# Forgetting attention: fill steps held to places between the heads, and the value product in exact high and low parts with both parts of the values in one stationary operand

## The chip, the core and the metric

The kernel runs on one core of a Trainium2 chip. The metric is the device time of one execution in microseconds; the median of several runs is compared. Engines are named as in the profile: PE (TensorE), DVE (VectorE), ACT (ScalarE), POOL (GpSimd), and SP, whose queue issues nearly all the loads.

## The reference, cut to what matters

One inference step of a decoder with two layers, for a prompt of 512 tokens and for eight samples of four new tokens each. Layer 0 is a state-space layer with sliding-window attention; layer 1 is the forgetting attention that this document is about. Each layer ends with a cross attention to 256 memory tokens and a feed-forward part. All is float32, model width 1024, 16 query heads in four key-value groups, 64 numbers a head.

```python
def fox_attend(q, k, v, cum, q_off):
    # Queries sit at key indices q_off..q_off+Tq-1; logit[t,s] += cum[t]-cum[s].
    ...
    bias = cq[..., :, None] - c[..., None, :]
    mask = jnp.arange(tk)[None, :] <= (q_off + jnp.arange(tq))[:, None]
    return gqa_attend(q, k, v, mask=mask, bias=bias)   # softmax(q k / 8 + bias) v

def fox_prompt(q, k, v, logf):
    cum = jnp.cumsum(logf, axis=1)
    ...  # blocks of 128 queries against all earlier keys

# the samples: 1024 earlier tokens, gathered by page, then the 4 new ones
kp = cache_fox_k[li, page_table].reshape(bs, past, FOX_KV_HEADS, HEAD_DIM)
vp = cache_fox_v[li, page_table].reshape(bs, past, FOX_KV_HEADS, HEAD_DIM)
```

## The kernel before

The whole network is recorded as one program for one core. A matrix product in full precision is made of exact parts: an operand is split into a high part (cast to the matmul's faster type, called fp32r in the profile) and a low part (the difference), and two or three products of the parts are summed in a bank of PSUM. `linear` and `linear_steps` do this for the weights: `pieces` loads a weight piece of 128x1024 on SP into a `room` tile (L158) and splits it, high part on ACT (L162), low part on DVE (L163), into a `split_t` tile.

In layer 1, `odd()` first makes keys, values and the queries of key-value groups 0 and 1 (four of the eight steps of the query projection). Then comes the stage that changes. It has two halves `m`, each with four blocks `c` of 128 queries, and in each block eight heads (`r` two key-value groups, `i` four query heads): 64 heads. Block c looks at W = 128(c+1) keys. A head goes like this:

- PE: two matmuls 128xW give the scores (`kh,qst` and `kl,qst`; the second half of the key rows carries the forget bias).
- DVE: a fused mask, negate and minimum from PSUM into `prt` (L1160).
- ACT: the exponential with its sum (L1161). DVE: the reciprocal (L1162). POOL: the scaling (L1163).
- Two heads later (FOX_AHEAD = 2), PE transposes the weights, c+1 times 128x128 (L141), and DVE or ACT in turn evict them to `PT` (L1143).
- After the block's last head the value product is made: float32 matmuls with 64 columns of V as the stationary operand and 512 columns of `PT` moving, for each key block and for r = 0, 1, the two r in the two column halves of the array. DVE copies the bank to `q` (L1150).

Around the heads, three generators give other work, a step at a time: "q", the other eight half-steps of the query projection (24 matmuls each, and an eviction at L456); "s", the samples' attention in four groups of two samples (`fox_sample`: 16 loads of 128 KB of keys, `fox_k`, and 16 of values, `fox_v`, for each group, at L1237, with the page numbers read by SP at L1233; scores by matmuls of 32 columns; softmax; transposes; value product); and "m", the keys and values of the cross attention's memory (`mem_begin` splits the memory at L251 and L252, then `mem_k` and `mem_v`). FOX_PLAN says after which head which generator takes a step. The order on each engine is then made by a scheduler, which may move work of a later step ahead of a head, or the other way round; `after()` adds an order of two instructions by hand.

PSUM banks have tags: "sc" (two buffers) for scores, "tr" (three), "tp" (two) for transposes, "pv" (one) for the value product. After the heads follows the output projection with `wo_d`; `hold` and `whold` keep its first splits and weight loads behind the eviction of the sixth block (`pvs[5]`).

Of the kernel before, what the change touches and what calls it, by code (L numbers as in the profile page):

```python
# [19 lines left out]
P = 128  # L20
# [19 lines left out]
FOX_PLAN = {}  # L40
for _a, _heads in (("q", range(4, 33, 4)), ("s", [33,34,36,38,40,41,43,45,47,49,51,53,55,57,59,61]), ("m", range(34, 64, 4))):
    for _h in _heads:
        FOX_PLAN[_h] = FOX_PLAN.get(_h, "") + _a
# [63 lines left out]
class Net:  # L107
    def __init__(self, nc, tc, ctx, I, O):
        self.nc, self.tc, self.ctx, self.I, self.O = nc, tc, ctx, I, O
        self.n = self.turn = 0  # L110
        self.hold = self.whold = self.last = None
# [25 lines left out]
    def mm(self, out, lhsT, rhs, start, stop):  # L137
        self.nc.tensor.matmul(out, lhsT, rhs, start=start, stop=stop)  # L138

    def tr(self, out, in_, k=P):  # L140
        self.nc.tensor.transpose(out, in_, self.ident[0:k, 0:k])  # L141

# [328 lines left out]

    def stack_q(self, Q, q, m, tok):

        nc = self.nc
        Q = Q.rearrange("p (r i t) -> p r i t", r=2, i=4)
        for r in range(2):
            a, b = slice(64 * r, 64 * r + 64), slice(64 - 64 * r, 128 - 64 * r)
            src = q.half(m)[a, :, tok]
            nc.scalar.copy(Q[a, r], src)
            nc.vector.tensor_tensor(Q[b, r], src, Q[a, r].bitcast(F32), ALU.subtract)  # L480
        return Q


# [504 lines left out]
    def odd(self, st, nxt, fill):  # L988
        nc, tc, I, O = self.nc, self.tc, self.I, self.O
        with ExitStack() as es:  # L990
# [53 lines left out]
            with tc.tile_pool(name="fox", bufs=1) as fx:  # L1044
                self.pvs = []
# [3 lines left out]
                K2 = self.fox_keys(kT, ncum)  # L1049
                bias = self.fox_bias(fx, klast)  # L1050
# [10 lines left out]
                next(gens["s"])  # L1061
                heads, ahead = 0, []
                for m in range(2):
                    for c in range(4):
                        for _ in self.fox_prompt(q, K2, V, m, c, ahead):
                            heads += 1
                            self.banks = ['sc'] if heads < 33 else ['sc', 'sc', 'tr']
                            for a in FOX_PLAN.get(heads, ""):
                                next(gens[a], None)
                self.fox_turn(ahead, 0)  # L1070
# [16 lines left out]
    def fox_keys(self, kT, ncum):  # L1087
# [20 lines left out]
        mask = self.prt[:, 4736:5248]  # L1108
        self.zero(mask[:, 0:384])
        self.after(nc.gpsimd.tensor_copy(mask[:, 384:512], self.cst[:, C_SWA + 128:C_SWA + 256]), self.last)  # L1110
        return kh, kl
# [13 lines left out]

    def fox_prompt(self, q, K2, V, m, c, ahead):

        nc = self.nc
        W = 128 * (c + 1)
        tok = slice(128 * c, 128 * c + 128)  # L1130
        Q = self.fox_queries(q, m, tok)
        PT = []
        mask = self.prt[:, 5248 - W:5248]

        def turn(pr, r, i):
            if not PT:
                PT.extend(self.H("PT")[:, 0:2048].rearrange("p (k r i t) -> p k r i t", k=2, r=2, i=4) for _ in range(c // 2 + 1))
            tp = self.psum("tp", [P, 4, 128])
            for kb in range(c + 1):
                self.tr(tp[:, kb], pr[:, 128 * kb:128 * kb + 128])  # L1140
            for u in range(c // 2 + 1):
                e = min(2, c + 1 - 2 * u)
                (nc.scalar.copy if i % 2 else nc.vector.tensor_copy)(PT[u][:, 0:e, r, i], tp[:, 2 * u:2 * u + e])  # L1143
            if (r, i) == (1, 3):
                pv = self.psum("pv", [P, 4, 128])
                for kb in range(c + 1):
                    for r in range(2):
                        g = 2 * m + r
                        self.mm(pv[64 * r:64 * r + 64], V[:, kb, 64 * g:64 * g + 64], PT[kb // 2][:, kb % 2, r], kb == 0, kb == c)
                self.pvs.append(nc.vector.tensor_copy(q.half(m)[:, :, tok], pv))  # L1150
        for r in range(2):
            for i in range(4):
                sc = self.bank([P, 512])
                for z in range(2):
                    self.mm(sc[:, 0:W], Q[z][:, r, i], K2[z][:, m, r, 0:W], z == 0, z == 1)
                nm, den, rec = self.ty(1), self.ty(1), self.ty(1)
# [63 lines left out]
    def fox_sample(self, q, kTs, Qb, ncs, V, lf, fx, S, sel):  # L1220
# [3 lines left out]
        keys, vals, page = {}, {}, {}  # L1224
        gate = kd = self.last

# [13 lines left out]
        load(keys, 0, "fox_k")  # L1240
        load(vals, 0, "fox_v")
        yield
        tp = self.psum("tp", [P, 16])
        self.mm(tp[0:32], self.Ub, lf[0:32, 4], True, True)
        nc.vector.tensor_scalar(ncs, tp[0:32].unsqueeze(2).to_broadcast([32, 16, 4]), -1.0, None, ALU.mult)
        self.sample_q(q, Qb)
        for G in range(4):
            sc = [self.psum("sc", [P, 4, 128]), self.psum("sc", [P, 4, 128])]
            sn = self.psum("tp", [P, 32])
            for u in range(2):  # L1250
                self.mm(sc[u].rearrange("p a b -> p (a b)"), sel[:, 128 * (G % 2):128 * (G % 2) + 128], S[:, G // 2, 512 * u:512 * u + 512], True, False)
                for b2 in range(2):
                    for m in range(2):
                        a = 64 * b2 + 32 * m
                        lq = Qb[:, 2 * G + b2, m].rearrange("p r i t -> p (r i t)")
                        self.mm(sc[u][a:a + 32], lq, keys[G, b2][:, 4 * u:4 * u + 4, 128 * m:128 * m + 128], False, True)
            for b2 in range(2):
# [5 lines left out]
                self.mm(sn[a:a + 64], ncs.rearrange("p h t -> p (h t)"), self.ident[0:32, 0:32], False, True)  # L1263
            wk = self.prt[:, 2560:4736]
            pr = wk[:, 0:1056]
            gate = nc.vector.tensor_tensor(pr[:, 1024:1056], sn, c[:, C_MN + 32 * G:C_MN + 32 * G + 32], ALU.add)
            if G < 3:
                load(keys, G + 1, "fox_k")
            yield
            mx, nm, den, d1, rec = self.ty(3), self.ty(1), self.ty(3), self.ty(1), self.ty(1)  # L1270
            for u in range(2):
                nc.vector.tensor_reduce(mx[:, u:u + 1], sc[u].rearrange("p a b -> p (a b)"), AX.X, ALU.max)
            nc.vector.tensor_reduce(mx[:, 2:3], pr[:, 1024:1056], AX.X, ALU.max)
            nc.vector.tensor_reduce(nm, mx, AX.X, ALU.max, negate=True)
            for u in range(2):
                nc.scalar.activation(pr[:, 512 * u:512 * u + 512], sc[u].rearrange("p a b -> p (a b)"), AF.Exp, bias=nm, accum_out=den[:, u:u + 1])
            nc.scalar.activation(pr[:, 1024:1056], pr[:, 1024:1056], AF.Exp, bias=nm, accum_out=den[:, 2:3])
            nc.vector.tensor_reduce(d1, den, AX.X, ALU.add)
            nc.vector.reciprocal(rec, d1)
            yield  # L1280
# [15 lines left out]
            nc.scalar.activation(Osb[:, 0], pv, AF.Copy, scale=rec)  # L1296
            self.sample_o(q, Osb, G, 1)
            if G < 3:
                load(vals, G + 1, "fox_v")
            yield  # L1300


    def mem_begin(self, l):
# [12 lines left out]
        for k in range(KD):  # L1316
            g = self.par[:, G_MEM + 8 * l + k:G_MEM + 8 * l + k + 1]
            self.split(mh, ml, raw[:, k], k, 0, 256, g)
            if first:
                self.square_acc(acc, raw[:, k], k, 256)  # L1320
        if first:
            self.rstd(acc, self.mcol, self.mb, [(0, 0, 128), (1, 128, 128)])
# [381 lines left out]
    def run(self):  # L1704
# [5 lines left out]
        def memory(l):  # L1710
            t = self.mkv = self.H("mkv")
            self.mk, self.mv = t[:, 0:1024].rearrange("p (h k) -> p h k", h=4), t[:, 1024:2048].rearrange("p (b f) -> p b f", b=2)
            nc.gpsimd.memset(t[:, 0:1], 0.0)
            m = self.mem_begin(l)
            yield from self.mem_k(l, m, self.mk)
# [128 lines left out]
```

## Time and profile before

| | |
|---|---|
| median of 3 runs | 1694.12 us (1693.13 to 1695.23) |
| profiled execution | 1698.67 us |
| span in its trace | 1696.9 us |
| mean granted TensorE clock | 0.990 |
| busy, share of the span | PE 97%, DVE 70%, ACT 46%, POOL 19% |
| loaded and stored | 189.27 MB, mean 112 GB/s |

Busy shares are of the whole program; a matmul's record includes time in which it waits inside the array's pipeline, so a busy PE need not be a fast one. The stage that changes lies between 1003 and 1190 us. In the trace an instruction is named by its line, its output and its inputs: `ps<-PT,odd` is the value product, `ps<-fox_k,odd` a sample's scores, `ps<-room,prt` a transpose. Lines are those of each kernel's own text, so the changed kernel's numbers differ from these.

### The profile page before, as it was taken

The page shows a single profiled execution, that of the slowest core. Times are in us where ns is not written, and L with a number is a line of the kernel's source. Part 1 is how long each engine was busy: PE and PEld are TensorE (multiplying, and loading weights), DVE is VectorE, ACT ScalarE, POOL GpSimd, SP SyncE. Part 2 cuts the span into 40 slices and gives each one's busy share as a digit, 9 for nine tenths or more (in the row PEclk, how much of TensorE's full clock was granted, in tenths as well). Part 3 has the DMA queues.
Part 4 walks back from the last instruction along what each step waited for, and adds up shares of the span by engine and source line. Part 5 has one row for each costly group of instructions (what it writes and reads, how often), then busy time and mean ns, then how long its engine had stood idle before and what let it go on. Part 6 is the DMA issues. An engine that isn't in the chain of part 4 may idle for free.

```text
span 1696.9 us, 32362 instructions
## 1 busy us (share of the span) xinstructions
PE 1645.9 (97%) x12720; PEld 1518.7 (89%) x12720; DVE 1184.0 (70%) x2296; ACT 778.3 (46%) x1603; POOL 328.3 (19%) x510
## 2 busy tenths in 40 slices
PE   6999999998999999999999998998999999999997
PEld 6988899886997999999999996655988999999997
DVE  7667678867766887677766567654567877777663
ACT  5255445344444544444445355544545444444444
POOL 5022312657422310000001203111223100000002
PEclk9999999999999999999999999999999999999999
DMA  5211424126533233232323334554551233223222
GB/s 185 63 55 39 145 82 132 51 91 237 207 100 125 81 113 102 89 103 88 106 75 107 127 116 125 160 174 149 181 178 59 75 113 100 94 100 106 75 68 86
DMA packets 71221, 189.27 MB, mean 112 GB/s; under 512 B 7612, under 2 KB 34012, under 8 KB 63452
## 3 DMA queue, kind: packets, MB, share of 16 engines
q1 hardware_dynamic: 69388, 184.84, 32.9%
q8 instruction: 100, 1.64, 0.4%
q10 hardware_dynamic: 1600, 1.83, 0.4%
q0 software_dynamic: 80, 0.52, 0.1%
q14 instruction: 53, 0.43, 0.1%
HBM read 172.22 MB, written 14.95 MB: 110 GB/s over the span
## 4 chain that ended last, share of the span: by engine, by line
PE 91%; DVE 3%; POOL 2%; ACT 1%; issue 1%; DMA 1%; SPq 0%; DVEq 0%; POOLq 0%; ACTq 0%
PE ps L138 66%; PE ps L1563 22%; PE ps L141 3%; POOL room L425 1%; DMA room<-wo_d 0%; POOL sq L421 0%; DVE split_t L1544 0%; ACT prt L1161 0%; DVE prt L1160 0%; DVE xs L879 0%; ACT split_t L162 0%; DMA mem<-mem 0%; DVE meml L252 0%; DVE x L1730 0%; DMA x<-x 0%
## 5 line engine op out<-in xcount | busy, mean ns | idle before, releaser
L138 PE MATMUL ps<-xh,split_t 128*128 128x288 f32 (+1 forms) x2304 | 463.8, 294 | 13.8 <-ACT split_t L162 11.8
L138 PEld LDWEIGHTS ps<-xh,split_t 128*128 128x128 f32 x2304 | 371.1, 190 | 19.8 <-ACT split_t L162 12.8
L1563 PE MATMUL ps<-xf,split_t 128*128 128x272 f32 x2592 | 348.9, 289 | 3.1 <-DVE split_t L1544 2.1
L138 PE MATMUL ps<-xl,split_t 128*128 128x256 f32 (+1 forms) x1152 | 339.1, 295 | 1.2 <-DVE xl L252 1.0
L1563 PEld LDWEIGHTS ps<-xf,split_t 128*128 128x128 f32 x2592 | 335.0, 188 | 4.4 <-DVE split_t L1544 3.0
L261 POOL TENSOR_TENSOR room<-room,sq 128x256 f32<-128x256 f32 (+1 forms) x96 | 86.4, 904 | 773.4 <-ACT sq L260 771.7
L138 PEld LDWEIGHTS ps<-xl,split_t 128*128 128x128 f32 x1152 | 218.9, 190 | 6.9 <-issue 4.3
L138 PE MATMUL ps<-hh,fs 128*128 128x256 f32 (+1 forms) x1024 | 206.3, 288 | 0.0
L162 ACT CAST split_t<-room 128x1024 fp32r<-128x1024 f32 (+1 forms) x128 | 130.3, 1019 | 156.5 <-PE ps L138 112.3
L163 DVE TENSOR_TENSOR split_t<-room,split_t 128x1024 fp32r<-128x1024 f32 (+1 forms) x128 | 157.0, 1229 | 31.5 <-ACT split_t L162 31.0
L138 PEld LDWEIGHTS ps<-hh,fs 128*128 128x128 f32 x1024 | 164.9, 188 | 0.4 <-ACT fs L1607 0.4
L1544 DVE TENSOR_TENSOR split_t<-fr,split_t 128x1024 fp32r<-128x1024 f32 x108 | 131.7, 1221 | 35.3 <-ACT split_t L1543 35.0
L1543 ACT CAST split_t<-fr 128x1024 fp32r<-128x1024 f32 x108 | 113.4, 1052 | 89.6 <-PE ps L1563 53.4
L138 PE MATMUL ps<-hl,fs 128*128 128x256 f32 (+1 forms) x512 | 147.3, 288 | 0.0
L138 PE MATMUL ps<-oh,split_t 128*128 128x288 f32 (+1 forms) x512 | 105.7, 298 | 1.3 <-ACT oh L246 1.2
L138 PEld LDWEIGHTS ps<-hl,fs 128*128 128x128 f32 x512 | 96.4, 188 | 0.0
L138 PEld LDWEIGHTS ps<-oh,split_t 128*128 128x128 f32 x512 | 83.2, 192 | 8.3 <-issue 5.0
L138 PE MATMUL ps<-ol,split_t 128*128 128x288 f32 (+1 forms) x256 | 77.1, 301 | 0.3 <-DVE ol L249 0.2
L1607 ACT CAST fs<-room 128x512 fp32r<-128x512 f32 x64 | 39.4, 618 | 82.6 <-PE ps L138 68.3
L252 DVE SCALAR_TENSOR_TENSOR xl<-x,room,xh 128x256 fp32r<-128x256 f32 (+1 forms) x96 | 69.6, 755 | 5.6 <-ACT xh L251 5.6
L138 PE MATMUL ps<-hh,split_t 128*128 128x256 f32 (+1 forms) x384 | 73.4, 288 | 0.0
L1620 DVE TENSOR_TENSOR x<-x,ps 128x256 f32<-128x256 f32 (+1 forms) x128 | 54.4, 433 | 26.9 <-PE ps L138 26.7
(423 smaller groups left out, 3091.2 us busy)
## 6 DMA issues: line engine op xcount, KB each, us to landing
fr<-wfi SPq DMA_DIRECT2D x36, 1024.0 KB
room<-wfo SPq DMA_DIRECT2D x64, 256.0 KB
room<-wo_e SPq DMA_DIRECT2D x16, 512.0 KB
xk<-mem_k SPq DMA_DIRECT2D x8, 1024.0 KB
xv<-mem_v SPq DMA_DIRECT2D x8, 1024.0 KB
room<-wfi SPq DMA_DIRECT2D x16, 512.0 KB
fox_k<-fox_k SPq DMA_DIRECT2D x64, 128.0 KB
fox_v<-fox_v SPq DMA_DIRECT2D x64, 128.0 KB
```

Source lines behind the costliest of these rows:

```text
L138: self.nc.tensor.matmul(out, lhsT, rhs, start=start, stop=stop)
L141: self.nc.tensor.transpose(out, in_, self.ident[0:k, 0:k])
L162: nc.scalar.copy(hi[:, 0:n], raw[:, 0:n])
L163: nc.vector.tensor_tensor(lo[:, 0:n], raw[:, 0:n], hi[:, 0:n].bitcast(F32), ALU.subtract)
L252: return nc.vector.scalar_tensor_tensor(ll, src, g, hh.bitcast(F32), ALU.mult, ALU.subtract)
L261: nc.gpsimd.tensor_tensor(acc, acc, sq[:, 0:N], ALU.add)
L425: nc.gpsimd.tensor_tensor(acc, acc, sq, ALU.add)
L1543: nc.scalar.copy(hi, t)
L1544: nc.vector.tensor_tensor(lo, t, hi.bitcast(F32), ALU.subtract)
L1563: self.nc.tensor.matmul(ps, w[a][:, k], x[:, b, k], start=start and k == 0 and i == 0, stop=k == 3 and i == 2, skip_group_check=True)
L1607: nc.scalar.copy(hi, raw)
L1620: nc.vector.tensor_tensor(x, x, ps, ALU.add)
```

## The change

Six edits, all in the forgetting attention:

1. **The plan.** FOX_PLAN has other places: the query steps at heads 2 to 24, the sample's at 8 and 25 to 58, the memory's at 19 to 60. `mem_begin` gives way after every second of its eight splits, in layer 1.
2. **Steps held.** The first PE instruction that a step records is ordered after the latest score matmul (`behind`, `placed`).
3. **Banks.** "tr" may have four buffers, "sc" three, and scores use both tags in all heads. (The scheduler places them in the same eight banks.)
4. **Queries.** The next block's queries are split half a block ahead.
5. **The value product.** V is stacked once as high and low part side by side, 128 columns, one stationary operand for each key block and r (`stack_v`). `PT` is evicted by whole banks into a high part (ACT, a cast) and a low part (DVE, the difference): a bank holds 4, 2, 1, 1 heads for c = 0 to 3. For each block and r, 2(c+1) fp32r matmuls with 512 columns give high and low sums in the two halves of the bank; ACT copies the one half (64x512), DVE adds the other. This is recorded one head later (`late`).
6. **The samples.** Scores go through a fused minimum reduce to SBUF as before in the prompt, and one exponential over 1056 columns takes the place of three. The first keys are loaded at head 8 and not before head 1, the first values at head 25, and the transposed result of a group is put into place a step later. The hold of the output projection is `pvs[11]`, the twelfth of now sixteen evictions.

```diff
-for _a, _heads in (("q", range(4, 33, 4)), ("s", [33,34,36,38,40,41,43,...,59,61]), ("m", range(34, 64, 4))):
+for _a, _heads in (("q", (2, 4, 7, 10, 13, 16, 20, 24)), ("s", (8, 25, 26, 28, 31, 33, ...)), ("m", (19, 21, 23, 25, 35, ...))):
...
-        bufs = {"tr": 3, "sc": 2, "tp": 2, "pv": 1}[tag]
+        bufs = {"tr": 4, "sc": 3, "tp": 2, "pv": 1}[tag]
...
+    def placed(self, i):
+        if self.behind is not None:
+            self.behind, d = None, self.behind
+            self.after(i, d)
+        return i
...
+    def stack_v(self, V, t):
+        ...
+        for r in range(2):
+            nc.scalar.copy(t[:, :, :, r, r], src[:, :, :, r])
+            nc.vector.tensor_tensor(t[:, :, :, r, 1 - r], src[:, :, :, r], t[:, :, :, r, r].bitcast(F32), ALU.subtract)
...
+    def turned(self, PT, tp):
+        self.nc.scalar.copy(PT[0], tp)
+        self.nc.vector.tensor_tensor(PT[1], tp, PT[0].bitcast(F32), ALU.subtract)
+
+    def values(self, q, V2, PT, r, blocks):
+        ...
+        for j, v in enumerate(blocks):
+            for z in range(2):
+                self.mm(pv, v[:, r], PT[z][j], j == 0 and z == 0, j == n - 1 and z == 1)
+        a, b = slice(64 * r, 64 * r + 64), slice(64 - 64 * r, 128 - 64 * r)
+        nc.scalar.copy(q[a], pv[b])
+        return nc.vector.tensor_tensor(q[a], pv[a], q[a], ALU.add)
...
-                self.banks = ['sc']
+                self.banks = ['sc', 'sc', 'tr']
...
+                    for _ in self.fox_prompt(Q, q, K2, V2, m, c, ahead):
+                        heads += 1
+                        if heads % 8 == 4 and j < 7:
+                            nq = ready(*blocks[j + 1])
+                        for a in FOX_PLAN.get(heads, ""):
+                            self.behind = self.scored
+                            next(gens[a], None)
...
-                self.hold = self.whold = self.pvs[5]
+                self.hold = self.whold = self.pvs[11]
```

What it does to the order is shown at three places. First PE, the value product of the last block (`oh`, `ol` is the output projection that runs beside it). Before:

```order
5121 L138 MATMUL ps_13740<-PT_13556,odd 64x512
5122 L141 MATMUL ps_13702<-room,prt 128x128 x4
5133 L141 MATMUL ps_13726<-room,prt 128x128 x4
5134 L141 MATMUL ps_13733<-room,prt 128x128 x4
5135 L138 MATMUL ps_13740<-PT_13556,odd 64x512 x3
5136 L138 MATMUL ps_13740<-PT_13557,odd 64x512 x4
5137 L138 MATMUL ps_13902<-oh_1543_13763,split_t 128x288
```

(between 5122 and 5133 stand matmuls of the output projection and one more set of transposes), and now, for the second half of its heads:

```order
5153 L138 MATMUL ps_13912<-oh_1540_13804,split_t 128x256
5154 L138 MATMUL ps_13783<-PT_13693,Vs_10848 128x512
5155 L138 MATMUL ps_13943<-oh_1538_13794,split_t 128x288
5156 L138 MATMUL ps_13783<-PT_13694,Vs_10848 128x512
5157 L138 MATMUL ps_13783<-PT_13693,Vs_10848 128x512
5158 L138 MATMUL ps_13783<-PT_13694,Vs_10848 128x512
5159 L138 MATMUL ps_13783<-PT_13693,Vs_10848 128x512
5160 L138 MATMUL ps_13783<-PT_13694,Vs_10848 128x512
5161 L138 MATMUL ps_13783<-PT_13693,Vs_10848 128x512
5162 L138 MATMUL ps_13783<-PT_13694,Vs_10848 128x512
```

The first half-width matmul stood alone ahead of the others, and the other seven after the last transposes; now eight full-width ones stand nearly together for this r, and eight more for the other r earlier.

Second DVE, in the last block of the first half (c = 3; L1160 is L1209 now, L1162 is L1211, L1150 is L515, L1143 is L503 and an ACT cast at L502). Before, two heads:

```order
1317 L1160 ISA prt,ty_11959<-ps_11956,prt 128x512
1318 L1160 ISA ty_11959 128x1
1319 L1143 COPY PT_11901<-ps_11966 128x2x128
1320 L1143 COPY PT_11902<-ps_11966 128x2x128
1321 L1162 RECIPROCAL ty_11961<-ty_11960 128x1
1322 L1160 ISA prt,ty_11976<-ps_11973,prt 128x512
```

and now:

```order
1318 L1209 ISA prt,ty_12029<-ps_12026,prt 128x512
1319 L1209 ISA ty_12029 128x1
1320 L503 TENSOR_TENSOR PT_11865<-ps_11983,PT_11864 128x3x128
1321 L1166 CAST qst<-qst 64x512
1322 L1167 TENSOR_TENSOR qst<-q_1102_11137,qst 64x512
1323 L1211 RECIPROCAL ty_12031<-ty_12030 128x1
1324 L503 TENSOR_TENSOR PT_12009<-ps_12010,PT_12008 128x4x128
1325 L515 TENSOR_TENSOR q_1087_10885<-ps_12017,q_1087_10885 64x4x128
1326 L503 TENSOR_TENSOR PT_12009<-ps_12036,PT_12008 128x4x128
1331 L1209 ISA prt,ty_12236<-ps_12233,prt 128x512
```

Every head's transposes now come to DVE as one wide subtract, where every second head's came as copies, and query splits of the next block and sample softmax stand among them.

Third SP, the keys of the second group of samples (group 1) and the memory's value weights (`wxv`). Before:

```order
282 L1237 ISA
283 L1237 DMA fox_k_12256<-fox_k 128x256
284 L158 DMA room<-wxv 128x1024 x2
285 L1237 ISA
286 L1237 DMA fox_v_12474<-fox_v 128x256
```

and now:

```order
250 L1282 TENSOR_LOAD tab_12063
251 L1282 ISA x2
252 L165 DMA room<-wxv 128x1024 x2
253 L1286 ISA
254 L1286 DMA fox_k_12209<-fox_k 128x256
255 L1286 ISA
256 L1286 DMA fox_k_12209<-fox_k 128x256
```

The two weight loads stood behind the sixteen key loads, and stand ahead of them now. Further down, two of the loads of `wo_d` stand behind the first of the last sixteen value loads, where one pair stood behind all of them.

More of the change, by code (lines that the diff above doesn't have):

```diff
@@ L1057, in odd @@
                 self.take(q)
-                self.banks = ['sc']
+                self.banks = ['sc', 'sc', 'tr']
                 gens = {"q": self.linear_steps(wq, range(4, 8), KD, xh, xl, qe),
                         "s": self.fox_sample(q, kTs, Qb, ncs, V, lf, fx, S, sel), "m": fill()}
-                next(gens["s"])
                 heads, ahead = 0, []
[L1063 to L1070, printed above, removed]
+                blocks = [(m, c) for m in range(2) for c in range(4)]
+                ready = lambda m, c: self.fox_queries(q, m, slice(128 * c, 128 * c + 128))
+                Q = ready(*blocks[0])
+                for j, (m, c) in enumerate(blocks):
+                    for _ in self.fox_prompt(Q, q, K2, V2, m, c, ahead):
[5 more added lines that the diff above has]
+                            next(gens[a], None)
+                        self.behind = None
+                    Q = nq
+                for _ in range(FOX_AHEAD):
+                    next(gens["m"], None)
+                    self.fox_turn(ahead, len(ahead) - 1)
                 for a in "qsm":
@@ L1300, in fox_sample @@
             yield
+            self.sample_o(q, Osb, G, 1)
     def mem_begin(self, l):
```

101 lines of the change are left out of this document (57 added, 44 removed).

## The prediction

> **What bounds the kernel now.** I read the page first, then a table of stretches, then the waits of VectorE, then the chain of waits where the forgetting attention ends.
>
> ```profile
> core 0 of [0], span 1696.9 us
> ...
> PE 1645.9 (97%) x12720; PEld 1518.7 (89%) x12720; DVE 1184.0 (70%) x2296; ACT 778.3 (46%) x1603; POOL 328.3 (19%) x510
> ```
>
> TensorE carries the kernel as a whole. But 97% is an average, and PE records are stretched by waits, so I go to the stage that changes. Its 64 heads run in blocks of eight. Each head has one mask-and-min reduce at L1160; the view of that line has the first and the last start after the durations, for all 64 and then for the first heads of the second half (a block of 128 keys, the fifth of eight):
>
> ```profile
> L1160 DVE CUSTOM_DVE_ANT_0 prt<-ps,prt x64: 259/481/692, 1012.0 to 1177.0; 128x128 f32<-128x128 f32 x16, 128x256 f32<-128x256 f32 x16, 128x384 f32<-128x384 f32 x16, 128x512 f32<-128x512 f32 x16
> ```
> ```profile
> L1160 DVE CUSTOM_DVE_ANT_0 prt<-ps,prt x2: 271/276/281, 1068.8 to 1071.0; 128x128 f32<-128x128 f32 x2
> ```
>
> So heads 1 to 32 take 1012 to 1069. The last value product ends at 1186.9 (its row is below). I cut there.
>
> ```profile
> core 0: us, PE busy (x) PEld busy (x) DVE busy (x) ACT busy (x) POOL busy (x), PEclk, DMA share, GB/s
> 1012.00:1069.00 57.00, 52.02 (x323) 37.43 (x322) 43.67 (x152) 34.54 (x98) 18.34 (x37) 1.00 0.44 137
> 1069.00:1187.00 118.00, 110.52 (x872) 72.59 (x864) 64.42 (x217) 57.18 (x159) 17.94 (x33) 0.97 0.54 161
> 1092.00:1112.00 20.00, 18.78 (x114) 12.85 (x110) 11.03 (x38) 9.02 (x24) 2.42 (x5) 0.91 0.67 191
> 1150.00:1172.00 22.00, 17.94 (x159) 11.30 (x157) 11.62 (x37) 11.47 (x33) 2.57 (x4) 0.99 0.65 187
> 1187.00:1240.00 53.00, 51.76 (x408) 51.55 (x409) 33.20 (x55) 25.96 (x49) 15.34 (x16) 1.00 0.45 162
> ```
>
> The last row is the output projection after the heads: 408 matmuls of 256 or 288 columns in 51.76 us, 0.127 us each, or 0.47 ns a column; that is PE at its pace. In the first half of the heads PE starts only 323 matmuls in 57 us, so it is not the limit there, whatever its 52 busy us say. VectorE is the nearest to full, 43.67 of 57, and it takes its work in order. The second half has 64.42 of 118 on VectorE. There PE is the likelier limit, and it loses 118 − 110.52 = 7.5 us to recorded idle and 0.03 × 118 = 3.5 us to a lower granted clock: 11.0 us together.
>
> What VectorE waits for, first half and then second half:
>
> ```profile
> DVE ty L1162 <- ACT prt L1161: 7.0, 13, 1.0
> DVE q L456 <- PE ps L138: 2.7, 2, 1.6
> DVE q L1150 <- PE ps L138: 1.3, 3, 0.7
> ```
> ```profile
> DVE ty L1162 <- ACT prt L1161: 12.1, 18, 2.0
> DVE q L1150 <- PE ps L138: 10.7, 5, 3.8
> DVE PT L1143 <- PE ps L141: 5.8, 6, 1.7
> DVE split_t L163 <- ACT split_t L162: 5.1, 6, 3.3
> DVE mkv L1350 <- PE ps L138: 4.9, 1, 4.9
> ```
>
> In the first half, 7.0 of its 57 − 43.67 = 13.3 idle us are the reciprocal waiting for its own head's exponential: a latency that other work could fill. In the second half the waits are mostly for PE, which is at long pieces of fill.
>
> The chain of waits near the end of the heads:
>
> ```profile
> 1159.19 0.96 SPq L1237
> 1161.29 6.04 DMA room<-wo_d
> 1167.35 1.05 ACT split_t L162
> 1168.43 1.23 DVE split_t L163
> 1170.38 4.43 PE ps L138 x24
> ```
>
> The third load of the output weights is issued behind the last sample values (SPq L1237), and PE waits for it; 1150 to 1172 has 22 − 17.94 = 4.1 us of PE idle.
>
> **The change part by part.** Prices of what the stage does now (by line and shape, 1003 to 1187 us), and of its nearest relatives:
>
> ```profile
> L138 PE MATMUL ps<-PT,odd 128*64 128x512 f32 x80 | 28.6, 618 | 0.5 <-ACT PT L1143 0.5
> L138 PE MATMUL ps<-fox_k,odd 128*32 128x512 f32 x64 | 13.5, 604 | 0.0
> L1143 DVE COPY PT<-ps 128x256 f32<-128x256 f32 x32 | 12.9, 419 | 6.5 <-PE ps L141 6.4
> L1143 ACT COPY PT<-ps 128x256 f32<-128x256 f32 x32 | 11.0, 371 | 27.4 <-PE ps L141 25.9 <-PE ps L138 1.4
> L1143 DVE COPY PT<-ps 128x128 f32<-128x128 f32 x16 | 4.6, 285 | 1.5 <-PE ps L138 1.1 <-PE ps L141 0.3
> L1143 ACT COPY PT<-ps 128x128 f32<-128x128 f32 x16 | 4.2, 261 | 1.3 <-PE ps L141 1.3
> L1150 DVE COPY q<-ps 128x512 f32<-128x512 f32 x8 | 5.5, 692 | 12.0 <-PE ps L138 12.0
> L1272 DVE TENSOR_REDUCE ty<-ps 128x1 f32<-128x512 f32 x8 | 5.5, 689 | 2.8 <-PE ps L138 2.7
> L252 DVE SCALAR_TENSOR_TENSOR meml<-mem,room,memh 128x256 fp32r<-128x256 f32 x8 | 3.4, 466 | 0.0
> ```
> ```profile
> L1421 ACT CAST Ph<-ps x16: 577/586/592, 507.7 to 1284.2; 128x512 fp32r<-128x512 f32 x16
> L1422 DVE TENSOR_TENSOR Pl<-ps,Ph x16: 673/692/693, 509.6 to 1284.9; 128x512 fp32r<-128x512 f32 x16
> ```
> ```profile
> 1183.25 3.65 PE L138 MATMUL ps<-PT,odd 128*64 128x512 f32 x14 [0.46 <-ACT PT L1143]
> ```
> *Evictions of the transposed weights.* Before, VectorE and ScalarE shared them: 12.9 + 4.6 = 17.5 us and 11.0 + 4.2 = 15.2 us. After, every bank is cast by ScalarE and subtracted by VectorE. Banks per key-value head and block: 1, 2, 4, 4 for the four block lengths, so 28 of 512 columns and 16 of 384. The cross attention does just this pair: 0.692 and 0.586 us. For 384 columns I go down by a line from 0.692 to 0.466 at 256 columns: 0.58 us. VectorE: 28 × 0.692 + 16 × 0.58 = 28.7, +11.2 us; ScalarE: 28 × 0.586 + 16 × 0.48 = 24.1, +8.9 us.
>
> *Evictions of the product.* 8 copies (5.5 us) become 16 ScalarE copies and 16 VectorE adds of 64x512. At the 0.692 and 0.586 above: VectorE +5.5 us, ScalarE +9.4 us. Stacking the values (two subtracts, two copies) lies ahead of the heads, where PE is full (the projection of the first queries): 0, at most 1.4 us if that cover is gone.
>
> *The product on PE.* Before, 40 fp32 matmuls of 64 columns, two records each. The last product's trailing 14 records (7 matmuls) take 3.65 us for four pairs of column halves, 0.91 a pair slot. The order puts one half alone ahead in each block, so a block of n key blocks takes n + 1 slots: 28 in all, 25.5 us. After: 80 matmuls 128x512 at 0.47 ns a column, 0.24 each, 19.3 us. Gain 6.2 us, half of it, 3.1, in the second half of the heads; in the first half VectorE hides it. Bounds: no lone slots, 20 × 0.91 = 18.2 us, a loss of 1.1; every record by itself, 28.6 us, a gain of 9.3. The Trainium skill, page "TensorE: Matmul & The Clock Gate", Part 3 on packing, says that matmuls in different column tiles run concurrently, the span being one matmul's duration and about 4 ns for each further tile. That speaks against the change: by it the old halves cost 18.2 us, and my sum would end 3.7 us later. The 80 records of 618 ns sum to 49 us in 28.6 us of PE time, so the trace agrees for the pairs; the order says that not all are pairs.
>
> *Sample scores.* 64 matmuls of 32 columns in 13.5 us, four at a time: 0.84 us a foursome. In the new order the foursomes are broken into twos for three of the four sample groups, before for two: two foursomes more, +1.7 us on PE. The two max-reduces of 0.689 become fused reduces of 512 columns at 0.692: 0.
>
> *Steps moved, first half.* The eight query steps are in heads 1 to 32 in both orders, but eight splits of the memory (0.466 each, 3.7 us) and one more reduce of sample scores (0.7) now come there too. VectorE's additions there: half the weights' 11.2 (5.6), half the product's 5.5 (2.8), 3.7 and 0.7: 12.8 us, 43.67 + 12.8 = 56.5. To this comes idle time: 13.3 at most, as now; about 4 at least, if all the waits for ScalarE (7.0) and for the product (1.3) are filled. I take 7.5, since longer VectorE work between a head's reduce and its reciprocal fills the 7.0 us mostly, while waits for PE stay. So 64 us against 57: **+7.0**, from +3.5 to +12.8. ScalarE then has 34.54 + 9.2 = 44 of 64 and stays covered.
>
> *Steps held, second half.* VectorE has 64.42 of 118; the additions (8.4) less what moved out (4.4) leave it at 68, so it costs nothing there as long as steps are spread. Each step's first PE instruction waits for the latest scores, so behind it queue the later transposes and products on PE; its price is the wait for a score bank, and one more bank each is allowed. What can be won is the 11.0 us of idle and clock; the upper end is 21, an estimate: the forms of the second half at 0.47 ns a column come to some 97 of the 118 us. On SP, two of the output-weight loads now stand behind the first of the last 16 value loads, so the 6-us wait should be out of the chain: 4.1 of the 11. The rest is the clock (0.91 from 1092 to 1112), and gaps that the held steps should split. I take all **11.0**; ends 0 and 21.
>
> Sum: 7.0 − 3.1 + 1.7 − 11.0 = −5.4 us. The profiled execution took 1698.67 (1.8 of it outside the span), 4.6 above the median of the runs; against its own time this gives 1693.3, against the median 1694.12 it gives 1688.7. I say **1688.5**.
>
> **Rivals.**
>
> *VectorE decides throughout (slower).* If the latency is not filled, the first half costs 56.5 + 13.3 = 69.8 us, +12.8. For it: 32 of the 44 banks belong to blocks of 384 and 512 keys, and their subtracts stand in order between the reduces. Then the transposes' bank comes free late, the held steps wait behind it, and the second half wins only the 4.1 of the weights and 1.4 on PE: +7.3, 1701.5. It decides once VectorE's idle time in the first half stays above 12.9 with the full 12.4 won later. Against: in the first half 12.4 us of idle are named waits that more queued work can cover.
>
> *Keys late (slower or same).* The loads of the sample's keys:
>
> ```profile
> 1104.92 15.56 SPq L1237 DMA_DIRECT2D fox_k<-fox_k  x16
> 1133.00 16.13 SPq L1237 DMA_DIRECT2D fox_k<-fox_k  x16
> ```
>
> They take some 16 us where the page numbers are read in between, and in the new order group 1's stand behind two loads of memory weights, of which the second waits for a VectorE split. From their step (head 28) to their use (head 34) are six heads, 6 × 64 / 32 = 12 us. Three groups each 4 us late cost 12, of which the old order had some; I price it at +9: 1697.5.
>
> *The product is no cheaper on PE.* By the concurrent halves: 3.1 + 0.6 us are lost, 1692, no change. *All stalls go:* +3.5 and −21 + 1.7 − 3.1: 1675.
>
> **How the numbers follow.** Forecast 0.36, all stalls 0.10, VectorE 0.24, keys late 0.16, product no cheaper 0.14. A measurement of this kernel tells a change from none at about 0.2%, 3.4 us. Faster: 0.46. Same: the product's case and some of the keys': 0.18. Slower: 0.36. The forecast's own range is 1683 to 1692; with the rivals of both signs 1676 to 1705.
>
> **What would show it.** Right: the 32nd head's reduce some 64 us after the first; the casts and subtracts near 0.586 and 0.692; the second half near 106 us at a granted clock of 0.99; no wait for output weights in the chain. The product right: 80 records spaced near 0.24. Wrong: PE waiting for sample keys (DMA in the waits of L138), VectorE above 90% in either half, ScalarE's copy of the product holding the one product bank, or the second half above 112 us.

## The result, and the profile after

The changed kernel takes 1709.06 us (median of four, 1707.15 to 1713.49) where the kernel before takes 1694.26 (four runs): ratio 1.0097, interval 1.0077 to 1.0116. It is slower by 14.8 us; 1688.5 was forecast, with 1705 as the upper end. Measured again beside other versions it came to 1.0089 (1.0071 to 1.0107), so 0.9% is the size to explain.

The first fence is a line of the changed kernel's page. The second has the first reduces of the second half (first and last start after the durations). The third has the stretches: first half, second half, and the output projection after the heads.

```profile
PE 1644.6 (96%) x12720; PEld 1531.2 (90%) x12720; DVE 1200.3 (70%) x2306; ACT 795.9 (47%) x1601; POOL 329.3 (19%) x510
```
```profile
L1209 DVE CUSTOM_DVE_ANT_0 prt<-ps,prt x2: 272/272/273, 1074.8 to 1075.7; 128x128 f32<-128x128 f32 x2
```
```profile
core 0: us, PE busy (x) PEld busy (x) DVE busy (x) ACT busy (x) POOL busy (x), PEclk, DMA share, GB/s
1009.30:1074.80 65.50, 58.47 (x372) 47.77 (x372) 54.59 (x168) 45.90 (x111) 19.22 (x37) 0.95 0.41 121
1074.80:1197.40 122.60, 104.34 (x827) 76.24 (x827) 69.40 (x209) 61.38 (x140) 18.37 (x33) 0.94 0.52 165
1197.40:1251.00 53.60, 53.10 (x418) 52.65 (x418) 33.40 (x55) 26.54 (x50) 15.35 (x16) 1.00 0.42 138
```

The heads took 57.0 + 118.0 = 175.0 us and take 65.5 + 122.6 = 188.1, 13.1 more. PE's recorded work is the same, 162.5 before and 58.47 + 104.34 = 162.8 now. So nearly all of the 13.1 us is recorded idle time of PE: 175.0 − 162.5 = 12.5 us before, 25.3 now. And the clock is lower: 0.05 × 65.5 + 0.06 × 122.6 = 10.6 us of granted clock are missing, where 3.5 were.

A profile is one execution, and the heads differ between executions. The profiled one of the kernel before, at 1698.67 us, is 4.4 above its median; the bank counts alone, which change nothing in time (e17 below), have heads of 171.9 us in their profile, 56.8 and 115.1. The changed kernel profiled a second time (e12), in an execution 5.9 us above its median, has 192.8:

```profile
1009.30:1077.20 67.90, 61.60 (x381) 50.56 (x380) 54.67 (x167) 46.17 (x111) 18.89 (x37) 0.90 0.38 117
1077.20:1202.10 124.90, 105.37 (x833) 76.73 (x832) 69.53 (x209) 61.35 (x140) 18.22 (x33) 0.95 0.52 162
```

So differences of less than some 5 us between the halves of two profiles below show a direction at most; the ratios decide.

What PE waits for in the second half: matmuls in the first fence, weight loads in the second. "issue" is time for which the profile names no cause.

```profile
PE ps L138 <- DVE ty L1209: 5.2, 8, 2.5
PE ps L138 <- DMA fox_k<-fox_k: 3.4, 3, 2.0
PE ps L141 <- DVE ty L1209: 2.8, 2, 2.4
PE ps L138 <- DVE PT L503: 1.6, 3, 0.8
```
```profile
PEld ps L138 <- issue: 14.7, 25, 2.2
PEld ps L138 <- DVE ty L1209: 8.0, 10, 2.7
PEld ps L138 <- DVE PT L503: 3.7, 5, 1.3
PEld ps L141 <- DVE ty L1209: 3.5, 2, 2.8
```

The same two views of the kernel before, second half, had for the reduce:

```profile
PE ps L138 <- DVE ty L1160: 0.7, 2, 0.5
```
```profile
PEld ps L138 <- DVE ty L1160: 1.9, 5, 0.8
```

The two views overlap in time and are not to be added, but both say the same: PE now waits for VectorE's reduces in the half where it hardly did, and a little for the new subtracts (L503). Over both halves the matmuls' wait for reduces grew less, from 4.8 us before (4.1 of them in the first half) to 10.0.

The row does not say why a reduce is late. Two waits, of 2.46 and 2.40 us, make 4.9 of the 8.0 (5.2 and 2.8) of the second half. The second, with what VectorE did ahead of it:

```profile
1169.90 1.23 DVE L170 TENSOR_TENSOR split_t<-room,split_t 128x1024 fp32r<-128x1024 f32 x1 [1.20 <-ACT split_t L169]
1171.04 0.55 DVE L503 TENSOR_TENSOR PT<-ps,PT 128x384 fp32r<-128x384 f32 x1
1172.32 1.97 PE L141 MATMUL ps<-room,prt 128*128 128x128 f32 x8 [2.40 <-DVE ty L1209]
```

VectorE waited 1.20 us for ScalarE's part of a split of the output weights and split for 1.23 us itself; one subtract of 0.55 us stands behind that, then the reduce. Ahead of the 2.46 (it ends at 1104.71) VectorE had a reduce of sample scores (0.69 us), a weight split (1.22), the split of the next block's queries (0.42 and 0.69) and a wait of 0.24 for the samples' long exponential, and no subtract at all. The longest wait of the first half, 2.59 us for L515, stands behind all eight splits of the memory in a row (3.34 us), though their step gives way after every second one. So the longest waits come from the other work between the heads more than from the subtracts.

The new evictions and the product by shape (1003 to 1198 us):

```profile
L138 PE MATMUL ps<-PT,Vs 128*128 128x512 f32 x80 | 26.0, 441 | 4.2 <-ACT PT L502 2.0 <-DVE ty L1326 1.0 <-DVE PT L503 0.5
...
L503 DVE TENSOR_TENSOR PT<-ps,PT 128x512 fp32r<-128x512 f32 x28 | 18.9, 686 | 1.8 <-ACT PT L502 1.5
...
L502 ACT CAST PT<-ps 128x512 fp32r<-128x512 f32 x28 | 15.9, 583 | 9.8 <-PE ps L141 8.0 <-DMA fox_k<-fox_k 1.6
...
L514 ACT COPY q<-ps 64x512 f32<-64x512 f32 x16 | 9.3, 581 | 15.1 <-PE ps L138 14.9
L503 DVE TENSOR_TENSOR PT<-ps,PT 128x384 fp32r<-128x384 f32 x16 | 8.6, 550 | 0.5 <-ACT PT L502 0.5
```

### The profile page after: what moved, and what is told of

Same layout as the page of the kernel before. It is cut to its first block, busy times and chain, and to the rows that moved or that the text cites. A ratio compares the mean times of both kernels' runs of the same rounds, so it can differ in the third digit from the quotient of the medians.

```text
span 1708.4 us, 32362 instructions
## 1 busy us (share of the span) xinstructions
PE 1644.6 (96%) x12720; PEld 1531.2 (90%) x12720; DVE 1200.3 (70%) x2306; ACT 795.9 (47%) x1601; POOL 329.3 (19%) x510
## 4 chain that ended last, share of the span: by engine, by line
PE 87%; DVE 5%; issue 2%; SPq 2%; POOL 2%; ACT 2%; DMA 1%; DVEq 0%; ACTq 0%; POOLq 0%
PE ps L138 63%; PE ps L1614 22%; PE ps L141 2%; SPq L1286 1%; POOL room L432 1%; SPq L1282 1%; DVE prt L1209 0%; DVE PT L503 0%; ACT split_t L169 0%; POOL sq L428 0%; DVE split_t L1595 0%; DMA mem<-mem 0%; DVE xs L913 0%; DMA room<-wo_d 0%; DVE q L515 0%
```

## The experiments

Each ratio is to the kernel before, measured with it on the same chip. Every edit also lets the scheduler make another order, so a ratio holds the edit and what that does to the order.

| run | what it is | ratio | interval |
|---|---|---|---|
| e1 | before + new product | 1.0083 | 1.0068 to 1.0097 |
| e2 | changed, old product | 1.0025 | 1.0015 to 1.0036 |
| e3 | changed, steps not held | 1.0131 | 1.0114 to 1.0148 |
| e4 | changed, keys in two loads | 1.0107 | 1.0094 to 1.0120 |
| e5 | changed, no subtracts | 1.0046 | 1.0028 to 1.0064 |
| e6 | changed, 40 matmuls for 80 | 1.0080 | 1.0062 to 1.0098 |
| e7 | changed, keys a group earlier | 1.0112 | 1.0092 to 1.0131 |
| e8 | changed, two product banks | 1.0079 | 1.0057 to 1.0101 |
| e9 | e2, memory's steps later | 1.0054 | 1.0034 to 1.0074 |
| e10 | e2, samples' steps later too | 1.0049 | 1.0031 to 1.0067 |
| e11 | changed, high part only | 1.0019 | 1.0002 to 1.0037 |
| e12 | changed, again | 1.0089 | 1.0071 to 1.0107 |
| e13 | before + new samples' part | 1.0290 | 1.0267 to 1.0312 |
| e14 | e2, old bank counts | 1.0177 | 1.0155 to 1.0199 |
| e15 | e2, steps not held | 1.0032 | 1.0019 to 1.0045 |
| e16 | before + new product, high part only | 0.9980 | 0.9965 to 0.9994 |
| e17 | before + new bank counts | 1.0000 | 0.9985 to 1.0014 |
| e18 | e16 + new bank counts | 0.9994 | 0.9980 to 1.0007 |

**The product alone, and everything but the product.** e1 takes `stack_v`, `turned`, `values` and the new `turn` into the kernel before; e2 puts the old `turn` into the changed kernel:

```diff
-            if i % nh == nh - 1:
-                self.turned([t[:, :, i - nh + 1:i + 1] for t in PT], bank[0])
...
+            for u in range(c // 2 + 1):
+                e = min(2, c + 1 - 2 * u)
+                (nc.scalar.copy if i % 2 else nc.vector.tensor_copy)(PT[u][:, 0:e, r, i], tp[:, 2 * u:2 * u + e])
```

> The kernel before with the exact-part value product alone (edit 5: stacked values, whole-bank casts and subtracts, one head later, the hold on the twelfth of sixteen evictions); plan, banks and samples as before. Theory D (the added evictions on VectorE and ScalarE cost the time): the first half of the heads grows from 57 us to about 65, the whole kernel by 8 to 14 us over before, to 1702-1708. Theory K (sample keys late under the new plan) or H (steps held make PE wait): within 3 us of before, since neither the plan nor the holding is in it.

> The changed kernel with the old value product (fp32, 64 columns, copies by both engines, hold on the sixth of eight evictions); plan, held steps, banks, queries and samples as changed. Theory D: about 1697, 12 us below the changed kernel. Theories K and H: 1706 to 1711, no gain, as the keys and the held steps stay.

e1 is 0.83% slower than before, e2 only 0.25%. The product makes most of the loss, in either plan. Halves of e1 and of e2, cut as above:

```profile
1010.20:1070.40 60.20, 50.06 (x319) 41.19 (x321) 49.41 (x151) 42.26 (x103) 18.07 (x37) 0.97 0.36 110
1070.40:1193.30 122.90, 106.45 (x866) 78.17 (x858) 74.26 (x221) 67.23 (x165) 17.85 (x33) 0.94 0.51 155
```
```profile
1004.90:1071.50 66.60, 63.25 (x420) 48.68 (x420) 51.90 (x171) 40.88 (x109) 19.50 (x37) 1.00 0.44 133
1071.50:1183.70 112.20, 100.91 (x780) 63.81 (x778) 56.28 (x202) 48.52 (x131) 17.83 (x33) 0.94 0.51 161
```

The product alone (e1) costs 3.2 us in the first half and 4.9 in the second. The rest of the change alone (e2) costs 9.6 in the first half and wins 5.8 in the second: PE does 420 matmuls in the first half instead of 323, so the steps were moved there and paid for there. Together (the changed kernel) the second half loses the gain and 4.6 more: 10.4 us separate it from e2's. These halves are set against a profile that is 4.4 us above its median, and the 8.1 us of e1 are short of its 0.83%, 14 us; against e17's halves e1 costs 3.4 and 7.8, and e2 costs 9.8 and wins 2.9.

In e1's second half the wait for reduces (L1195 there) is small, and waits for ScalarE lead, for a cast (L496) and for exponentials of the samples (L1311):

```profile
PE ps L138 <- ACT PT L496: 3.3, 1, 3.3
PE ps L141 <- ACT prt L1311: 2.5, 1, 2.5
PE ps L138 <- DVE ty L1195: 1.0, 2, 0.5
```

So the product costs as much where PE hardly waits for reduces in this half. Those waits are not the one chain by which it costs.

**Holding the steps.** The one line that names the score is taken out:

```diff
                         for a in FOX_PLAN.get(heads, ""):
-                            self.behind = self.scored
                             next(gens[a], None)
```

> The changed kernel without the order between a step's first PE instruction and the latest score. Theory H: 8 us or more below the changed kernel, about 1700. Theories D and K: within 3 us of 1709.

> e2 without the order between a step and the latest score. With the new product the holding was worth 6 us (e3 against the changed kernel). If it is worth as much here: 1.0055 or more. If holding only helps where VectorE is late: within 2 us of e2's 1.0025, or below it.

Not holding them is slower (e3), so the holding is not the cause. With the old product it makes no difference that can be measured (e15 against e2). Theory H (the held steps make PE wait) falls.

**Keys.** In e4 the keys of groups 1 to 3 come in two large loads from fixed pages, which leaves out the page table; in e7 they are loaded a group earlier:

```diff
+        load(keys, 1, "fox_k")
...
-            if G < 3:
-                load(keys, G + 1, "fox_k")
+            if G < 2:
+                load(keys, G + 2, "fox_k")
```

> The changed kernel, in which the keys of sample groups 1 to 3 come from fixed pages in two loads of 1 MB each instead of sixteen of 128 KB after sixteen page numbers (it leaves out the page table for these keys). Theory K: 8 to 12 us below the changed kernel, 1697 to 1701, the second half of the heads near 112 us. Theories D and H: within 3 us of 1709.

> The changed kernel with the sample keys loaded one group earlier: groups 0 and 1 ahead, group G+2 once group G's scores are made. Theory K (keys late, 3.4 us of PE waits named for them and more behind): 4 to 8 us below the changed kernel. Theories D2, P, B: within 3 us of 1709.

No gain in either. e4 is no clean test, as its two loads were queued behind others and a wait for keys was left. In e7 the wait for keys is

```profile
PE ps L138 <- DMA fox_k<-fox_k: 2.6, 2, 2.4
```

where 3.4 stood, and the time is not lower. Neither edit takes the wait away, so neither is a clean test. The better evidence is e1 and e2: e1 keeps the old plan and its loads and still loses 0.83%; e2 keeps the new plan and its loads, its PE still waits 2.5 us for keys in the second half, and it loses 0.25%. Keys are late now and then, but they are not the 14 us.

**Inside the product.** e5 drops the 44 subtracts and puts the high part in the place of the low one, e6 drops the 40 matmuls with the low part of the weights, e11 both; e8 gives the product a second bank.

```diff
     def turned(self, PT, tp):
         self.nc.scalar.copy(PT[0], tp)
-        self.nc.vector.tensor_tensor(PT[1], tp, PT[0].bitcast(F32), ALU.subtract)   # e5, e11
...
-            for z in range(2):
-                self.mm(pv, v[:, r], PT[z][j], j == 0 and z == 0, j == n - 1 and z == 1)
+            self.mm(pv, v[:, r], PT[0][j], j == 0, j == n - 1)                         # e6, e11
```

> The changed kernel without the 44 VectorE subtracts that make the low part of the transposed weights; the high part is used in both products (it leaves out the low part, and keeps all 80 wide matmuls and all ScalarE casts). Theory D2 (VectorE's subtracts, in order between a head's reduce and its reciprocal, keep the second half of the heads long): 9 us or more below the changed kernel, 1700 or less. Theory P (the 80 wide matmuls cost PE more than the old product) and B (the one product bank): within 3 us of 1709.

> The changed kernel with half of the product's matmuls: the product with the low part of the weights is left out, 40 matmuls in place of 80; all evictions stay. Theory P: 40 x 0.23 = 9 us below the changed kernel, about 1700. Theory D2: PE is not what is late, at most 3 us below, 1706 to 1709.

> The changed kernel without the low part of the weights at all (it leaves out the 44 subtracts of e5 and the 40 matmuls of e6). If subtracts and matmuls are two prices of one product, it comes to e2's ratio, 1.002 to 1.003; if the matmuls only fill time in which PE waits anyhow, to e5's, 1.0046; if ScalarE's casts and copies (33 us where 15 stood) carry most, it stays above 1.005.

> The changed kernel with two banks allowed for the value product. Theory B (each product waits until ScalarE's copy and VectorE's add of the one before have freed the one bank): 4 us or more below the changed kernel. Theories D2, P, K: within 3 us of 1709.

> The changed kernel itself, as the measure for the others on one chip: 1.0097 of before, within 1.0077 to 1.0116; PE idle near 25 us between the first reduce and the last product, where the kernel before has 12.

From 1.0089 (e12), the subtracts are worth 0.43% (7 us), the matmuls by themselves 0.09%, which the intervals do not tell from nothing; both together 0.70% (12 us). That is e2's ratio, so what is left of the product, with its casts and copies but also with 40 wide matmuls in place of the old 40 of two records each, comes to no more than the old one. Half the wide matmuls, some 9 us of PE, bring next to nothing while the subtracts are there. Halves of e6 and of e11:

```profile
1008.10:1077.40 69.30, 63.20 (x416) 52.48 (x414) 58.23 (x172) 47.96 (x115) 18.25 (x37) 0.93 0.37 115
1077.40:1192.90 115.50, 97.28 (x755) 67.22 (x756) 65.29 (x205) 58.55 (x137) 17.73 (x33) 0.91 0.52 157
```
```profile
1007.10:1071.40 64.30, 59.76 (x407) 49.41 (x407) 48.59 (x154) 47.60 (x114) 19.41 (x37) 0.97 0.46 140
1071.40:1178.60 107.20, 90.44 (x750) 64.44 (x751) 50.99 (x180) 59.19 (x138) 17.71 (x33) 0.95 0.51 158
```

In e6 VectorE has 58.23 + 65.29 = 123.5 us, as much as the changed kernel's 124.0, and the heads take 184.8, of which PE is idle for 24.3 (25.3 in the changed kernel), with 0.07 × 69.3 + 0.09 × 115.5 = 15.2 us of clock missing (10.6). PE's recorded work is 160.5 us for 162.8, so the matmuls left out show neither as time won nor as more idle time. In e11 VectorE has 99.6 us and the heads take 171.5, in an execution of 1691.83 us that is 5.5 below its median. A second product bank (e8) brings nothing that can be measured.

**The plan's places.** With the old product, e9 starts the memory's steps at head 29; e10 starts them at 32 and also puts off the samples' steps (its plan is shown):

```diff
-("s", (8, 25, 26, 28, 31, 33, ...)), ("m", (19, 21, 23, 25, 35, 37, 39, 46, 54, 60))
+("s", (8, 25, 31, 33, 35, 36, ...)), ("m", (32, 34, 36, 38, 40, 41, 44, 48, 54, 60))
```

> The changed kernel with the old value product (as in e2) and the memory's steps put off, to heads 29 to 60 in place of 19 to 60. Theory M (work moved into the first half is what lengthens it there, 66.6 us in e2): the first half falls to about 62 and the whole by 3 us or more, to 1694 or less. Rival (the work only comes back in the second half): first half about 62, the whole within 2 us of e2.

> As e9, with the samples' steps put off too (8, 25, then 31 to 58) and the memory's at 32 to 60, so that heads 1 to 30 have only query steps and two loads beside them, as in the kernel before. Theory M: first half 57 to 60 us, the whole below the kernel before, 1690. Rival: first half 57 to 60 us, the whole within 2 us of e2, near 1697.

```profile
1006.50:1069.30 62.80, 56.41 (x369) 42.44 (x368) 49.09 (x168) 38.52 (x107) 19.07 (x37) 0.99 0.40 126
1069.30:1191.00 121.70, 109.92 (x828) 71.18 (x828) 59.78 (x207) 52.05 (x133) 17.94 (x33) 0.92 0.52 157
```

e10's first half is 3.8 us shorter than e2's, not the 7 to 10 that were expected, and its second half is 9.5 longer. In e9 the halves are 65.2 and 119.9, so that its first half hardly moved. Both kernels are slower than e2, e9 by 0.29% and e10 by 0.24%, with intervals that overlap a little. Theory M, by which the whole would gain, falls: work moved into the first half is paid for there and saves more later.

**The other pieces.** e13 is the samples' part alone in the kernel before, e14 e2 with three and two banks, e17 the bank counts alone in the kernel before:

> The kernel before with the samples' part of the change alone (fused reduces, one exponential over 1056 columns, the first values loaded later, the result put into place a step later); plan, banks, product as before. If the samples' part is what makes e2 slower: 3 us or more above before. Else within 3 us of it.

> e2 (changed kernel with the old product) with the old bank counts, three and two. If the greater counts cost (eight banks are shared by more tags): 2 us or more below e2's ratio of 1.0025. If they help the held steps: 3 us or more above. Else within 2 us.

> The kernel before with the new bank counts alone (four and three for three and two). If the counts by themselves help or cost: more than 3 us from before, to either side. If they only matter with the other edits: within 3 us of it.

The counts alone do nothing (e17). e13 and e14 lose 49 and 30 us, far more than the 4 us of e2 that they were to divide, so they do not answer the question. e13's first reduce starts at 1022.5 and its heads take 202.5 us, and no run says why. In e14 the first reduce starts at 1020.4 and in e2 at 1004.9, so half of the 29 us between the two lies ahead of the attention: the bank counts hold for the whole program, and so does the order that the scheduler makes of it (e14 first, then e2):

```profile
L1203 DVE CUSTOM_DVE_ANT_0 prt<-ps,prt x64: 270/480/693, 1020.4 to 1192.8; 128x128 f32<-128x128 f32 x16, 128x256 f32<-128x256 f32 x16, 128x384 f32<-128x384 f32 x16, 128x512 f32<-128x512 f32 x16
```
```profile
L1203 DVE CUSTOM_DVE_ANT_0 prt<-ps,prt x64: 269/478/692, 1004.9 to 1172.6; 128x128 f32<-128x128 f32 x16, 128x256 f32<-128x256 f32 x16, 128x384 f32<-128x384 f32 x16, 128x512 f32<-128x512 f32 x16
```

**The old plan without the low part.** e16 is e1 without the low part of the weights, e18 the same with the new bank counts.

> The kernel before with the wide product, high part of the weights alone (it leaves out the 44 subtracts and the 40 matmuls with the low part, as e11; old plan). By e11 against e12 (0.7% between them) it comes 11 to 12 us below e1's 1.0083: 1.0005 to 1.002, about before. If the old plan's gaps hide less of ScalarE's casts: 1.003 or more.

> e16 (old plan, wide product with the high part of the weights alone; it leaves out the low part) with the new bank counts. If more banks let PE run ahead of VectorE's reduces: 3 us or more below e16's 0.998. Else within 3 us of it.

e16 is 0.2% faster than before and the only one below it beyond its interval, and 1.03% (17 us) faster than e1, more than the 12 that were expected; the price is a product without the low part of the weights. e18, in which only the bank counts differ, is not told from before, so the 0.2% is near what can be told at all. Against e1 the result is clear: the low part costs in the old plan as in the new one. e16's halves:

```profile
1010.30:1066.10 55.80, 46.77 (x307) 38.17 (x305) 39.96 (x133) 42.28 (x103) 19.11 (x37) 0.97 0.42 128
1066.10:1178.50 112.40, 103.29 (x842) 74.33 (x834) 59.91 (x195) 66.02 (x165) 17.86 (x33) 0.92 0.53 165
```

ScalarE has 42.28 + 66.02 = 108.3 us there, 16.6 more than before's 91.7, and the heads still take 6.8 us less (168.2 for 175.0; 3.7 less than e17's 171.9). This does not show that ScalarE's casts and copies are free: PE has 150.1 us of work for 162.5 and VectorE 99.9 for 108.1, which may pay for them, and in e1 PE does wait for a cast. No run adds or takes away ScalarE's part alone.

## Why the prediction was wrong, point by point

- *Prices of the evictions.* Right: subtracts 0.686 and 0.550 us (0.692 and 0.58 were taken), casts 0.583, copies 0.581.
- *First half.* 64 us forecast, 65.5 measured (67.9 in e12), with VectorE busy 54.6 of 56.5 forecast. The nearness is in part luck, as the parts were off. The additions were put at 8.4 us of evictions and 4.4 of moved work. The runs show 3.2 for the product alone (e1) and 9.6 for the rest alone (e2): moved PE work (323 matmuls before, 372 now) was not priced. The least idle time, "about 4", does not come out of its rows either: 13.3 − 7.0 − 1.3 is 5.0.
- *The product on PE.* 26.0 us of PE for 28.6, and its records are at 0.23 spacing (seven in 1.77 us, the last lasting 0.39: (1.77 − 0.39) / 6):

```profile
1195.62 1.77 PE L138 MATMUL ps<-PT,Vs 128*128 128x512 f32 x7
```

  So 80 of them come to 18.4 us, near the 19.3 forecast. The gain of 3.1 us in the second half was counted as time; e6, where 9 us of such matmuls less bring nothing that can be measured, speaks against that.
- *Steps held, second half: this step failed.* It said that VectorE "costs nothing there as long as steps are spread" and took all 11.0 us of idle and clock as won. VectorE's load was forecast well, 68 us for 69.4; its price of nothing was wrong. Measured: idle went from 7.5 to 18.3 us and missing clock from 3.5 to 7.4, so the 11.0 that were to go became 25.7. The half took 122.6 us where 105.6 were forecast, and that 17 is nearly the whole miss of 20.6. A busy share of 0.55 was read as room. That the product's low part costs is shown in both plans, 12 us by e11 and 17 by e16; that the subtracts carry 7 of the 12 is shown by e5, in the new plan alone. That a subtract costs by standing ahead of the next head's reduce in VectorE's order is argued. Without the product (e2) the half wins 5.8 of the 11.0, or 2.9 against e17.
- *The output weights* were to leave the chain of waits, worth 4.1 of the 11.0. They did not, and the wait of 2.40 us above stands behind them; in the changed kernel's chain stands

```profile
1164.00 4.74 DMA room<-wo_d
```

- *Rivals.* "VectorE decides throughout" had 0.24 and came nearest: 1701.5 was its price, too low by 7.6, because it still let the second half win 5.5. It was near in number and engine and not in its mechanism: by its own condition idle time of VectorE above 12.9 us in the first half decides, and 65.5 − 54.6 = 10.9 were measured; most of the miss came in the second half. "Keys late" had 0.16 and is not the cause, by e1 and e2, though its sign, PE waiting for sample keys, did show. That the old halves ran concurrently, so that the product is no cheaper, was tested by no run.

What stays open is by which chain the low part holds PE. The waits for the reduces do not settle it: e1 has 1.0 us of them in its second half, and in e5, without any subtract, that half still has

```profile
PE ps L138 <- DVE ty L1208: 7.3, 4, 4.5
```

so that this wait has another source. How much of each price is the order that the scheduler made is open too, as are the 4 us that e2 loses and the losses of e13 and e14.

## What to carry to other kernels

A busy share does not say that an engine has room. VectorE was busy for 55% of the second half, and the subtracts added to its work still cost about 7 us: look at what stands in its order ahead of the instruction that the bottleneck waits for, and what that in turn waits for. A row of waits names the last instruction, not the late one, so follow the longest of them back. PE work taken away need not buy time (e6); find first what makes PE wait, here by leaving out the subtracts and the matmuls one at a time and then both. An edit that is good by itself may be undone by another, so the two halves of a change should be timed apart (e1 and e2), and an edit that makes a scheduler reorder the program is timed with that order.

## What the hardware showed that was not expected

The granted clock fell without a long gap, but not where the averages suggest. In the changed kernel from 1108 to 1131 us it was 0.86, while PE had 19.90 busy of 23 us, in pieces:

```profile
1108.00:1131.00 23.00, 19.90 (x164) 13.40 (x163) 11.69 (x39) 10.09 (x22) 2.30 (x5) 0.86 0.48 144
```

In finer stretches the clock in the heads of both kernels is 0.50 or 1.00 and nothing between, and the 0.86 is a mixture: 0.50 from 1104.1 to 1114.3, and 1.00 from there to 1131, although PE waits for 0.66, 0.82 and 0.97 us in that part. Its spells at 0.50 last about 3.4 us, or three times that here. The fall at 1104.1 came within the wait of 2.46 us that ends at 1104.71, and the one at 1172.3 at the end of the wait of 2.40; a wait of 2.01 us that ends at 1152.61 brought none. In the kernel before, the clock fell at 1100.0, and in the 10 us ahead of that PE had been idle for 0.71 in all.

No named wait of PE in the whole second half is longer than 2.5 us (the row of 8 waits for L1209 above). The Trainium skill, page "TensorE: Matmul & The Clock Gate", Part 1, section "HAM oscillation", gives as the rule "no PE-idle gaps >~3.4µs"; by that alone this clock would have stayed up, and the measurement decides against it. The page's next section, on a second failure mode, says that in another kernel frequent short idle times between groups of matmuls also made the clock change to and fro; the falls after short waits are of that kind, but from 1114.3 to 1131 PE idles in short pieces at full clock, so these traces do not show how much idle time it takes. Nor is a lower clock by itself the loss: e16 lacks 0.03 × 55.8 + 0.08 × 112.4 = 10.7 us of clock, as much as the changed kernel, and is the fastest of all.
